# Moving every SBUF tile of a four-layer decoder trunk to a common byte offset, and the split weights to eight others

## The chip, the cores and the metric

The kernel runs on one core of a Trainium2 chip. The metric is the device time of one execution in microseconds (us). Before the change the median of two runs is 2387.1 us (2386.57 and 2387.62). The profile and the rows below come from one further execution of 2388.11 us.

## The reference

A decoder trunk of four pre-norm residual layers works on a sequence of 512 positions with 1024 features, all in float32. Layer i mixes tokens with differential attention (layers 0 and 3), stick-breaking attention (layer 1) or sliding-window attention (layer 2), and each mixer is followed by a gated MLP of 2 x 2752 hidden features with a causal convolution of width 3:

```python
for layer in range(DEPTH):
    h = rmsnorm(x, attn_norm[layer])
    m = mixer(h)                      # qkv = h @ w_qkv, attention
    x = x + m @ w_o[layer]
    h = rmsnorm(x, ffn_norm[layer])
    u = conv(h @ w_up[layer]) + conv_b[layer]
    gate, val = split(u)
    x = x + (silu(gate) * val) @ w_down[layer]
return rmsnorm(x, final_norm)
```

The output is the whole 512 x 1024 array.

## The kernel before

Activations lie transposed: a tile has 128 features as partitions and the 512 positions as columns, so x is eight pieces of 128x512. To keep float32 accuracy with the fp32r matmul, each operand is split into a high part (rounded to fp32r by a copy) and a low part (the rest), and each product is three matmuls: high times high, high times low, low times high. The helper `mm3` (lines 497 to 500) issues them. In it the first operand after the output is the stationary one, loaded as 128x128 weights, and the next is the moving one, streamed through the array, mostly 512 columns.

**The weights** come from HBM in pieces of 128x512 float32 (four 128x128 blocks side by side) through four buffers `w_raw`. For each piece ScalarE writes a copy into one of four buffers `w_hi` (line 288) and VectorE writes the difference into one of four buffers `w_lo` (line 291). The buffers go round in rings, so a high tile and a low tile of the same number serve together, for twelve matmuls as a rule: four blocks times three. The ring order is fixed when the program is written out.

**The stages.** In each layer the q, k and v projections and the attention are interleaved on TensorE. Projections to q and k, and the up-projection of the MLP, move `h_hi` and `h_lo` (the normed x, split) against weights from `w_hi` and `w_lo`. The projections to v (line 561) do it the other way round: `w_hi` and `w_lo` are moved in 256 columns, and blocks of `h_hi` and `h_lo` are the weights. Then `out_projection` (line 1207) moves the attention's output `oh`, `ol`, and `feed_forward` (line 1228) moves the activated hidden features `gh`, `gl`, 21 pieces for each of eight outputs plus a last half piece (`gt_hl` against `wt_hi` and `wt_lo`, lines 1348 and 1349). The last output of the last layer is made in two halves of 256 columns.

**The order of the work** is written out by a planner: `Clock` (line 147) keeps an estimated time for each engine and decides by it in which order instructions are emitted. Its costs do not know addresses.

**Where tiles lie.** `pool.tile` lays the tiles of a pool one behind the other, each size rounded up to 32 bytes; an attention pool and a feed-forward pool take turns in the same space above the constants, and a tile of the new pool may be written only when the last reader of what lay there is done. An address below is bytes within a partition, and an offset is the address modulo 256. In the kernel before:

| tiles | offset |
|---|---|
| `w_raw`, `w_hi`, `w_lo`, `x`, `h_hi`, `h_lo`, `r_bc` | 192 |
| `acc`, `acc_h`, `acc_l`, `ones_r`, `tmp`, `ident`, `sbm` | 224 |
| `oh`, `ol`, `gh`, `gl`, `gt_hl` | 128 |
| `wt_hi`, `wt_lo`, the five `y` | 224 |
| matmul operands inside attention (`qs`, `ql`, `ks`, `vh`, `vl`, `at`) in layers 0, 2 and 3 | 0 |
| matmul operands inside attention (`qs`, `ql`, `ks`, `vh`, `vl`, `ah`, `al`) in layer 1 | 128 |

Blocks and pieces inside a tile are 512 or 2048 bytes apart, so they have their tile's offset.

Of the kernel before, what the change touches and what calls it, by code (L numbers as in the profile page):

```python
# [11 lines left out]
F32 = mybir.dt.float32  # L12
F32R = mybir.dt.float32r
# [4 lines left out]
P = 128  # L18
T = 512
D = 1024  # L20
ND = D // P
NB = T // P
DEPTH = 4
D_FF = 2752
NFF = D_FF // P
# [4 lines left out]
N_BUCKETS = 32  # L30
# [17 lines left out]
def lambda_init(layer):  # L48
    return 0.8 - 0.6 * math.exp(-0.3 * layer)


def f(ap):
    return ap.bitcast(F32)


def flat(ap):
    return ap.rearrange("p k m -> p (k m)")
# [15 lines left out]
def mm(*ns, prio=0):  # L73
    return PE, sum(max(n / 2.4, 107.0) for n in ns), prio


def act(n, prio=0):
    return ACT, 95 + 0.83 * n, prio


def dve(n, ops=1, prio=0):
    return DVE, ops * (70 + 1.04 * n), prio
# [14 lines left out]
def pool_dma(prio=0):  # L97
    return POOL, 1000.0, prio
# [48 lines left out]
class Clock:  # L147
# [7 lines left out]
    def spawn(self, gen):  # L155
        task = Task(gen, self)
        self.todo.append((task, None))
        return task
# [60 lines left out]
def trunk(ctx: ExitStack, tc: tile.TileContext, A, out):  # L219
    nc = tc.nc  # L220

    const = ctx.enter_context(tc.tile_pool(name="const", bufs=1))
# [3 lines left out]
    clock = Clock()  # L226
# [3 lines left out]
    def event():  # L230
        return Event(clock)

    def ring(pool, name, bufs, shape=(P, T), dtype=F32):
        return Ring(clock, [pool.tile(list(shape), dtype, name=f"{name}_{i}") for i in range(bufs)])

    banks = ring(psp, "ps", 8)

    def load_const(name):
        ap = A[name]
        t = const.tile(list(ap.shape), F32, name=f"c_{name}")  # L240
        nc.gpsimd.dma_start(out=t, in_=ap)
        return t

    pinned = "natural_log_exp_and_others"
    nc.scalar.preload_act_table_set(pinned)
    gains = load_const("gains")
    eps = const.tile([P, 1], F32, name="eps")
    nc.vector.memset(eps, EPS)


    stream = []
    raws = ring(const, "w_raw", 4)
    w_hi = ring(const, "w_hi", 4, dtype=F32R)
    w_lo = ring(const, "w_lo", 4, dtype=F32R)
    used = [0]

    def stream_rows(w, pieces):
# [54 lines left out]
        w_lo.give(w[1])  # L312


    xa = const.tile([P, ND, T], F32, name="x")
    x = [xa[:, d, :] for d in range(ND)]
    h_hi = [const.tile([P, T], F32R, name=f"h_hi{d}") for d in range(ND)]
    h_lo = [const.tile([P, T], F32R, name=f"h_lo{d}") for d in range(ND)]
    r_bc = const.tile([P, T], F32, name="r_bc")
    r_col = const.tile([P, NB], F32, name="r_col")  # L320
    acc = const.tile([P, T], F32, name="acc")
    acc_h = const.tile([P, T], F32R, name="acc_h")
    acc_l = const.tile([P, T], F32R, name="acc_l")
    ones_r = const.tile([P, P], F32R, name="ones_r")
    nc.vector.memset(acc[:, 0:P], 1.0 / P)
    nc.vector.tensor_copy(ones_r, acc[:, 0:P])
    tmps = ring(const, "tmp", 3)
# [156 lines left out]
    spawn(w_feed(first))  # L484

    ident = load_const("ident")
    sbm = const.tile([P, 2, P], F32R, name="sbm")
    tri_r, rest_r = (sbm[:, i, :] for i in range(2))
    sinks = const.tile([P, 16], F32, name="sinks")
    nc.gpsimd.dma_start(out=sinks, in_=A["sinks"].to_broadcast([P, 16]))  # L490
    subln = load_const("subln")
    sb_mask = load_const("sb_mask")
# [184 lines left out]

    rows_da = dram.tile([16, DA_Y], F32, name="rows_da")
    rows_sw = dram.tile([16, SW_Y], F32, name="rows_sw")
    neg_lam = const.tile([P, 2], F32, name="neg_lam")  # L680
    neg_sinks = const.tile([P, 16], F32, name="neg_sinks")
    subln_s = const.tile([P, 2], F32, name="subln_s")
    tables = event()

    def setup_tables(pool, big, small):
        def const_in(name, r):
            ap = A[name]
            n = math.prod(ap.shape[1:])
            t = yield r
            v = t if len(t.shape) == 2 else flat(t)  # L690
            yield pool_dma()
            nc.gpsimd.dma_start(out=v[0:ap.shape[0], :n], in_=flat(ap) if len(ap.shape) == 3 else ap)
            return t, v[0:ap.shape[0], :n]

        t0, onehot_da = yield from const_in("onehot_da", big)
        t1, onehot_sw = yield from const_in("onehot_sw", small)
        tab = pool.tile([N_BUCKETS + 1, 16], F32, name="tab")
        yield dve(16)
        nc.vector.memset(tab, 1.0)
        yield pool_dma()  # L700
        nc.gpsimd.dma_start(out=tab[0:N_BUCKETS], in_=A["rel_bias"])
        t2, masks = yield from const_in("sb_masks", small)
        lam_t = yield small
        yield pool_dma()
        nc.gpsimd.dma_start(out=lam_t, in_=A["lam"].to_broadcast([P, 512]))
        yield DMA_LAT
        for rows, oh, n, t, r in ((rows_da, onehot_da, DA_Y, t0, big), (rows_sw, onehot_sw, SW_Y, t1, small)):
            sbt = yield big
            sb = flat(sbt)
            for c in range(0, n, T):  # L710
                e = min(n, c + T)
                ps = yield banks.spare(1)
                yield mm(4 * (e - c), prio=-1)
                nc.tensor.matmul(ps[0:16, 0:e - c], tab, oh[:, c:e], start=True, stop=True)
                yield LAT
                yield dve(e - c)
                nc.vector.tensor_copy(sb[0:16, c:e], ps[0:16, 0:e - c])
                banks.give(ps)
            r.give(t)
            yield pool_dma(-1)  # L720
            nc.gpsimd.dma_start(out=rows, in_=sb[0:16, 0:n])
            clock.t += DMA_LAT
            big.give(sbt)
        yield DMA_LAT
        tables.set()
        yield dve(256)
        nc.vector.tensor_copy(flat(sbm), masks)
        small.give(t2)
        lam = lam_t.rearrange("p (l j e) -> p l j e", l=2, j=4)
        prod_t = yield small  # L730
        prod = prod_t[:, 0:256].rearrange("p (l j e) -> p l j e", l=2, j=2)
        dots = pool.tile([P, 2, 2], F32, name="lam_dots")
        yield dve(128, 2)
        for j in range(2):
            nc.vector.tensor_tensor(prod[:, :, j], lam[:, :, 2 * j], lam[:, :, 2 * j + 1], ALU.mult)
        small.give(lam_t)
        yield dve(256)
        nc.vector.tensor_reduce(dots, prod, mybir.AxisListType.X, ALU.add)
        small.give(prod_t)
        yield act(4)  # L740
        nc.scalar.activation(dots, dots, AF.Exp)
        yield dve(16, 5)
        for s in range(2):
            li = lambda_init(3 * s)
            nc.vector.scalar_tensor_tensor(neg_lam[:, s:s + 1], dots[:, s, 1:2], -li, dots[:, s, 0:1], ALU.add, ALU.subtract)
            nc.vector.tensor_scalar(subln_s[:, s:s + 1], subln[:, s:s + 1], 1.0 - li, None, ALU.mult)
        nc.vector.tensor_scalar(neg_sinks, sinks, -1.0, None, ALU.mult)
# [478 lines left out]


    def feed_forward(pool, l, norm, nxt):
        gh = pool.tile([P, NFF, T], F32R, name="gh")
        gl = pool.tile([P, NFF, T], F32R, name="gl")  # L1230
        gt_hl = pool.tile([P, T], F32R, name="gt_hl")
        gt_l = pool.tile([64, T], F32R, name="gt_l")
        ut = ring(pool, "ut", 3, (P, T + 2))
        for _, _, t in ut.free:
            nc.gpsimd.memset(t[:, 0:2], 0.0)
        y_r = ring(pool, "y", 5)

        wt_hi = pool.tile([P, D], F32R, name="wt_hi")
        wt_lo = pool.tile([P, D], F32R, name="wt_lo")
        nc.gpsimd.memset(f(wt_lo)[64:P], 0.0)  # L1240
        g = [event() for _ in range(NFF)]
        wt = [event(), event()]
# [113 lines left out]
    spawn(norm.finish(True))  # L1356
    for l in range(DEPTH):
        with tc.tile_pool(name=f"att{l}", bufs=1, reuse_waits="tile") as pool:
            oh = pool.tile([P, ND, T], F32R, name="oh")
            ol = pool.tile([P, ND, T], F32R, name="ol")  # L1360
            done, last_bank = [event() for _ in range(ND)], event()
            nxt = Norm(2 * l + 1)
            if l % 3 == 0:
                tasks = diff_attention(pool, norm, l, l // 3, oh, ol, done, last_bank)
            elif l % 3 == 1:
                tasks = stick_attention(pool, norm, l, oh, ol, done, last_bank)
            else:
                tasks = window_attention(pool, norm, l, oh, ol, done, last_bank)
            tasks.append(spawn(out_projection(oh, ol, done, last_bank, nxt, tasks[int(l % 3 != 1)])))
            clock.run(tasks)  # L1370
            norm = nxt
            spawn(norm.finish(False))
        with tc.tile_pool(name=f"ffn{l}", bufs=1, reuse_waits="tile") as pool:
            last = l == DEPTH - 1
            nxt = LastNorm(2 * l + 2) if last else Norm(2 * l + 2)
            clock.run(feed_forward(pool, l, norm, nxt))
            norm = nxt
            if not last:
                spawn(norm.finish(True))
# [94 lines left out]
```

## Time and profile before

| | |
|---|---|
| median of the runs | 2387.1 us |
| profiled execution | 2388.11 us |
| its span, first to last instruction | 2386.3 us |
| TensorE matmul, instructions | 11271 |
| VectorE, ScalarE, GpSimd busy | 1620.2, 1225.1, 382.1 us |
| mean granted TensorE clock | 0.996 |

Matmuls are pipelined: the duration that the profile gives one overlaps the next. How fast TensorE goes through them is read from the distance between the starts of two matmuls in the timeline, divided by the matmuls between them, called the pitch here. The timeline gives starts to 0.01 us, so the pitch is taken over several matmuls.

### The profile page before, as it was taken

Reading aid. Unit: us, or ns where it says so; the run is one execution under the profiler, and the core shown is the slowest. Engines: PE = TensorE matmul, PEld = TensorE weight load, DVE = VectorE, ACT = ScalarE, POOL = GpSimd, SP = SyncE. Lnnn points to the kernel's source line nnn. Section 1 sums busy time; section 2 is a strip of 40 time slices with the busy share of each in tenths; the row PEclk is TensorE's granted clock in tenths of the full one; section 3 lists DMA queues with packets and bytes.
Section 4 is the critical chain, followed back from the end, with each engine's and each line's share of the span. In section 5 each row is a group of like instructions: output and inputs, shape, how many; then the busy total and the mean of one; then the engine's idle time right before and its main releaser. Section 6 shows DMA issues by size and latency. Waiting matters only on the chain.

```text
span 2386.3 us, 33050 instructions
## 1 busy us (share of the span) xinstructions
PE 2337.6 (98%) x11271; PEld 1943.6 (81%) x11271; DVE 1620.2 (68%) x3054; ACT 1225.1 (51%) x2413; POOL 382.1 (16%) x405
## 2 busy tenths in 40 slices
PE   8999999999999999999999899999999999999998
PEld 6888788888877887888888788888888887888887
DVE  6787877743499968777335858776336886877624
ACT  4665545433477755454335855454334665545433
POOL 3343200000144311000002320000012443000001
PEclk9999999999999999999999999999999999999999
DMA  5553333333333323333335423333335642333333
GB/s 188 157 151 94 98 98 106 98 90 92 124 102 93 99 67 98 98 106 94 93 92 151 129 67 104 96 106 93 93 113 143 156 137 71 108 99 103 95 90 108
DMA packets 144153, 256.34 MB, mean 107 GB/s; under 512 B 18511, under 2 KB 33519, under 8 KB 143984
## 3 DMA queue, kind: packets, MB, share of 16 engines
q1 hardware_dynamic: 139856, 241.57, 33.7%
q0 software_dynamic: 4128, 12.66, 2.1%
q8 instruction: 88, 1.44, 0.3%
q14 instruction: 81, 0.66, 0.1%
HBM read 212.15 MB, written 2.16 MB: 90 GB/s over the span
## 4 chain that ended last, share of the span: by engine, by line
PE 59%; DVE 5%; ACT 1%; DMA 1%; issue 1%; POOL 0%; SPq 0%; DVEq 0%; ACTq 0%; POOLq 0%
PE ps L499 18%; PE ps L500 18%; PE ps L498 18%; PE ps L561 2%; PE ps L675 1%; DVE w_lo L291 1%; DMA ks<-lo 1%; DVE h_lo L366 1%; DVE a L799 0%; ACT ns L783 0%; PE ps L1157 0%; DVE ns L779 0%; DVE vl L581 0%; PE ps L992 0%; DVE x L1203 0%
## 5 line engine op out<-in xcount | busy, mean ns | idle before, releaser
L288 ACT ACTIVATE w_hi<-w_raw 128x512 fp32r<-128x512 f32 (+2 forms) x775 | 477.6, 617 | 827.9 <-PE ps L499 665.7
L291 DVE TENSOR_TENSOR w_lo<-w_raw,w_hi 128x512 fp32r<-128x512 f32 (+2 forms) x775 | 538.5, 696 | 444.2 <-ACT w_hi L288 434.2
L498 PE MATMUL ps<-h_hi,w_hi 128*128 128x512 f32 x1840 | 721.9, 392 | 6.7 <-ACT h_hi L364 5.4
L500 PE MATMUL ps<-h_hi,w_lo 128*128 128x512 f32 x1840 | 718.7, 391 | 2.8 <-DVE w_lo L291 2.8
L499 PE MATMUL ps<-h_lo,w_hi 128*128 128x512 f32 x1840 | 720.5, 392 | 0.7
L499 PEld LDWEIGHTS ps<-h_lo,w_hi 128*128 128x128 f32 x1840 | 346.5, 188 | 78.1 <-DVE h_lo L366 9.5
L498 PEld LDWEIGHTS ps<-h_hi,w_hi 128*128 128x128 f32 x1840 | 346.6, 188 | 76.9 <-ACT h_hi L364 5.4
L500 PEld LDWEIGHTS ps<-h_hi,w_lo 128*128 128x128 f32 x1840 | 346.3, 188 | 75.7 <-DVE w_lo L291 3.2
L498 PE MATMUL ps<-gh,w_hi 128*128 128x512 f32 (+1 forms) x693 | 268.4, 387 | 0.0
L500 PE MATMUL ps<-gh,w_lo 128*128 128x512 f32 (+1 forms) x693 | 268.2, 387 | 0.0
L499 PE MATMUL ps<-gl,w_hi 128*128 128x512 f32 (+1 forms) x693 | 268.2, 387 | 0.0
L1249 DVE TENSOR_TENSOR ut<-ps,r_bc 128x512 f32<-128x512 f32 x172 | 118.5, 691 | 176.8 <-PE ps L500 176.8
L381 POOL TENSOR_TENSOR acc<-tmp,tmp 128x512 f32<-128x512 f32 x9 | 11.6, 1292 | 1036.4 <-ACT tmp L373 1032.6
L1254 ACT ACTIVATE y<-ut,c_conv 128x512 f32<-128x512 f32 x172 | 140.2, 815 | 44.0 <-DVE ut L1249 44.0
L499 PEld LDWEIGHTS ps<-gl,w_hi 128*128 128x128 f32 x693 | 129.6, 187 | 30.3
L500 PEld LDWEIGHTS ps<-gh,w_lo 128*128 128x128 f32 x693 | 129.7, 187 | 30.1
L498 PEld LDWEIGHTS ps<-gh,w_hi 128*128 128x128 f32 x693 | 129.6, 187 | 30.0
L1256 DVE SCALAR_TENSOR_TENSOR y<-ut,c_conv,y 128x512 f32<-128x512 f32 x172 | 128.5, 747 | 21.6 <-ACT y L1254 21.4
L1257 DVE SCALAR_TENSOR_TENSOR y<-ut,c_conv,y 128x512 f32<-128x512 f32 x172 | 129.3, 752 | 6.1
L381 POOL TENSOR_TENSOR acc<-acc,tmp 128x512 f32<-128x512 f32 x53 | 76.9, 1451 | 286.8 <-ACT tmp L373 243.1
L561 PE MATMUL ps<-w_hi,h_hi 128*128 128x256 f32 x416 | 119.2, 287 | 0.0
L561 PE MATMUL ps<-w_lo,h_hi 128*128 128x256 f32 x416 | 118.1, 284 | 0.0
(205 smaller groups left out, 3440.3 us busy)
## 6 DMA issues: line engine op xcount, KB each, us to landing
w_raw<-in_w_up_dram SPq DMA_DIRECT2D x344, 256.0 KB, 2.6
w_raw<-in_w_qk_dram SPq DMA_DIRECT2D x108, 256.0 KB, 2.8
w_raw<-in_w_down_dram SPq DMA_DIRECT2D x99, 256.0 KB, 2.6
w_raw<-in_w_down_dram SPq DMA_DIRECT2D x99, 192.0 KB, 2.3
qs<-hi SPq DMA_DIRECT2D x128, 128.0 KB, 3.1
w_raw<-in_w_o_dram SPq DMA_DIRECT2D x64, 256.0 KB, 2.7
w_raw<-in_w_v_dram SPq DMA_DIRECT2D x52, 256.0 KB, 2.8
ql<-lo SPq DMA_DIRECT2D x64, 128.0 KB, 3.0
```

The lines of the kernel that those rows point to most:

```text
L288: copy(hi[:, :n], raw[:, :n], AF.Copy)
L291: nc.vector.tensor_tensor(lo[:, :n], raw[:, :n], f(hi[:, :n]), ALU.subtract)
L366: nc.vector.scalar_tensor_tensor(h_lo[d], x[d], g, f(h_hi[d]), ALU.mult, ALU.subtract)
L381: nc.gpsimd.tensor_tensor(acc, self.first if n == 2 else acc, sq, ALU.add)
L498: nc.tensor.matmul(ps, wh, xh, start=start, stop=False, **kw)
L499: nc.tensor.matmul(ps, wh, xl, start=False, stop=False, **kw)
L500: nc.tensor.matmul(ps, wl, xh, start=False, stop=stop, **kw)
L561: nc.tensor.matmul(dst, a[:, ts], c[:, j, :], start=k + b + n == 0, stop=k == ND - 1 and n == 2, skip_group_check=True)
L1249: nc.vector.tensor_tensor(u[:, 2:T + 2], ps, r, ALU.mult)
L1254: nc.scalar.activation(y, u[:, 2:T + 2], AF.Identity, scale=cw[:, 2:3], bias=cw[:, 3:4])
L1256: nc.vector.scalar_tensor_tensor(y, u[:, 1:T + 1], cw[:, 1:2], y, ALU.mult, ALU.add)
L1257: nc.vector.scalar_tensor_tensor(y, u[:, 0:T], cw[:, 0:1], y, ALU.mult, ALU.add)
```

## The change

A small tile `home` and a helper `place` are new. `home` takes 64 bytes, after which the next address has offset 192. `place` allocates a tile and, behind it, an unused filler that brings the tile's size to a multiple of 256 bytes, so that the next tile has offset 192 again. All SBUF tiles are allocated through it, in the constants and in the pools, but for the eight tiles of split weights. These get unused fillers of 0, 128, 128, 32, 96, 128, 96 and 64 bytes in front of them, in the order of `w_hi` 0 to 3 and `w_lo` 0 to 3, and one of 96 bytes behind the last. Worked out from that, their offsets become:

| | 0 | 1 | 2 | 3 |
|---|---|---|---|---|
| `w_hi` | 192 | 64 | 192 | 224 |
| `w_lo` | 64 | 192 | 32 | 96 |

No instruction is added, removed or reordered; the operands' addresses alone differ. The core of the diff:

```diff
+    const.tile([P, 16], F32, name="home")
+
+    def place(pool, name, shape, dtype=F32):
+        t = pool.tile(list(shape), dtype, name=name)
+        gap = -(-(-4 * math.prod(shape[1:]) // 32) * 32) % 256
+        if gap:
+            pool.tile([P, gap // 4], F32, name=name + "_gap")
+        return t
+
     def ring(pool, name, bufs, shape=(P, T), dtype=F32):
-        return Ring(clock, [pool.tile(list(shape), dtype, name=f"{name}_{i}") for i in range(bufs)])
+        return Ring(clock, [place(pool, f"{name}_{i}", shape, dtype) for i in range(bufs)])
...
     raws = ring(const, "w_raw", 4)
-    w_hi = ring(const, "w_hi", 4, dtype=F32R)
-    w_lo = ring(const, "w_lo", 4, dtype=F32R)
+
+    apart = []
+    for i, gap in enumerate((0, 128, 128, 32, 96, 128, 96, 64)):
+        if gap:
+            const.tile([P, gap // 4], F32, name=f"w_apart{i}")
+        apart.append(const.tile([P, T], F32R, name=f"w_{'hl'[i // 4]}{i % 4}"))
+    const.tile([P, 24], F32, name="w_apart")
+    w_hi, w_lo = Ring(clock, apart[:4]), Ring(clock, apart[4:])
...
-    h_hi = [const.tile([P, T], F32R, name=f"h_hi{d}") for d in range(ND)]
-    h_lo = [const.tile([P, T], F32R, name=f"h_lo{d}") for d in range(ND)]
+    h_hi = [place(const, f"h_hi{d}", (P, T), F32R) for d in range(ND)]
+    h_lo = [place(const, f"h_lo{d}", (P, T), F32R) for d in range(ND)]
...
-        gh = pool.tile([P, NFF, T], F32R, name="gh")
-        gl = pool.tile([P, NFF, T], F32R, name="gl")
-        gt_hl = pool.tile([P, T], F32R, name="gt_hl")
-        gt_l = pool.tile([64, T], F32R, name="gt_l")
+        gh = place(pool, "gh", (P, NFF, T), F32R)
+        gl = place(pool, "gl", (P, NFF, T), F32R)
+        gt_hl = place(pool, "gt_hl", (P, T), F32R)
+        gt_l = place(pool, "gt_l", (64, T), F32R)
...
-            oh = pool.tile([P, ND, T], F32R, name="oh")
-            ol = pool.tile([P, ND, T], F32R, name="ol")
+            oh = place(pool, "oh", (P, ND, T), F32R)
+            ol = place(pool, "ol", (P, ND, T), F32R)
...
```

## Rows read from the trace of the kernel before

**Rows 1.** The page, part 1: busy us (share of the span), instructions.

```profile
PE 2337.6 (98%) x11271; PEld 1943.6 (81%) x11271; DVE 1620.2 (68%) x3054; ACT 1225.1 (51%) x2413; POOL 382.1 (16%) x405
```

**Rows 2.** Waits of TensorE, longest in total: waiter, releaser, us, times, longest.

```profile
PE ps L499 <- DVE al L971: 6.1, 9, 1.9
PE ps L988 <- DVE z L960: 5.4, 9, 1.3
```

**Rows 3.** Groups by line: output<-moving,weights, shape, count, busy us, mean ns, idle before.

```profile
L498 PE MATMUL ps<-h_hi,w_hi 128*128 128x512 f32 x1840 | 721.9, 392 | 6.7 <-ACT h_hi L364 5.4 <-ACT w_hi L288 1.3
L498 PE MATMUL ps<-gh,w_hi 128*128 128x512 f32 (+1 forms) x693 | 268.4, 387 | 0.0
L498 PE MATMUL ps<-oh,w_hi 128*128 128x512 f32 x256 | 102.1, 399 | 0.3 <-DVE nm L1068 0.3
L561 PE MATMUL ps<-w_hi,h_hi 128*128 128x256 f32 x416 | 119.2, 287 | 0.0
```

**Rows 4.** Timeline of TensorE in layer 0's up-projection: start, duration in us.

```profile
300.00 0.39 PE L500 MATMUL ps<-h_hi,w_lo 128*128 128x512 f32 x1
...
301.36 0.39 PE L500 MATMUL ps<-h_hi,w_lo 128*128 128x512 f32 x1
```

**Rows 5.** The same in layer 0's down-projection, also six matmuls apart.

```profile
500.00 0.39 PE L499 MATMUL ps<-gl,w_hi 128*128 128x512 f32 x1
...
501.40 0.39 PE L499 MATMUL ps<-gl,w_hi 128*128 128x512 f32 x1
```

**Rows 6.** The same in layer 0's output projection, six matmuls apart.

```profile
201.21 0.39 PE L498 MATMUL ps<-oh,w_hi 128*128 128x512 f32 x1
...
202.61 0.39 PE L498 MATMUL ps<-oh,w_hi 128*128 128x512 f32 x1
```

**Rows 7.** The same in a projection to v, 256 columns, twelve matmuls apart.

```profile
49.43 0.28 PE L561 MATMUL ps<-w_hi,h_hi 128*128 128x256 f32 x1
...
50.87 0.28 PE L561 MATMUL ps<-w_hi,h_hi 128*128 128x256 f32 x1
```

**Rows 8.** The same in the last half output, 256 columns, six matmuls apart.

```profile
2360.04 0.28 PE L499 MATMUL ps<-gl,w_hi 128*128 128x256 f32 x1
...
2360.72 0.28 PE L499 MATMUL ps<-gl,w_hi 128*128 128x256 f32 x1
```

**Rows 9.** The same where weights at offset 224 come between h's matmuls.

```profile
113.17 0.39 PE L499 MATMUL ps<-h_lo,w_hi 128*128 128x512 f32 x1
113.40 0.40 PE L500 MATMUL ps<-h_hi,w_lo 128*128 128x512 f32 x1
113.64 0.40 PE L846 MATMUL ps<-osh,ones_r 128*128 128x512 f32 x1
...
114.35 0.40 PE L499 MATMUL ps<-h_lo,w_hi 128*128 128x512 f32 x1
```

**Rows 10.** The same where four score matmuls (offset 0) come between h's.

```profile
65.60 0.39 PE L500 MATMUL ps<-h_hi,w_lo 128*128 128x512 f32 x1
65.83 0.39 PE L675 MATMUL ps<-ks,qs 128*128 128x512 f32 x1
...
66.75 0.39 PE L498 MATMUL ps<-h_hi,w_hi 128*128 128x512 f32 x1
```

**Rows 11.** Busy us (instructions) of each engine in 20 us of up- and down-projection.

```profile
300.00:320.00 20.00, 20.00 (x90) 16.57 (x89) 15.05 (x23) 9.25 (x15) 0.00 (x0) 1.00 0.29 92
500.00:520.00 20.00, 20.00 (x87) 16.07 (x86) 6.75 (x11) 6.29 (x11) 0.00 (x0) 1.00 0.35 96
```

**Rows 12.** Timeline of GpSimd where layer 3 begins: start, us, [idle before <-releaser].

```profile
1772.41 0.52 POOL L542 MEMSET ql<- 64x512 f32 x1
1781.20 1.50 POOL L771 DMA_DIRECT2D bias<-rows_da  x2 [8.27 <-PE ps L500]
1785.27 1.28 POOL L381 TENSOR_TENSOR acc<-acc,tmp 128x512 f32<-128x512 f32 x1 [2.57 <-ACT tmp L373]
```

More of the change, by code (lines that the diff above doesn't have):

```diff
@@ L239, in load_const @@
         ap = A[name]
-        t = const.tile(list(ap.shape), F32, name=f"c_{name}")
+        t = place(const, f"c_{name}", tuple(ap.shape))
         nc.gpsimd.dma_start(out=t, in_=ap)
@@ L246, in trunk @@
     gains = load_const("gains")
-    eps = const.tile([P, 1], F32, name="eps")
+    eps = place(const, "eps", (P, 1), F32)
     nc.vector.memset(eps, EPS)
@@ L312, in w_done @@
         w_lo.give(w[1])
-    xa = const.tile([P, ND, T], F32, name="x")
+    xa = place(const, "x", (P, ND, T), F32)
     x = [xa[:, d, :] for d in range(ND)]
-    h_hi = [const.tile([P, T], F32R, name=f"h_hi{d}") for d in range(ND)]
-    h_lo = [const.tile([P, T], F32R, name=f"h_lo{d}") for d in range(ND)]
[L319 to L324, printed above, removed]
+    h_hi = [place(const, f"h_hi{d}", (P, T), F32R) for d in range(ND)]
+    h_lo = [place(const, f"h_lo{d}", (P, T), F32R) for d in range(ND)]
+    r_bc = place(const, "r_bc", (P, T), F32)
+    r_col = place(const, "r_col", (P, NB), F32)
+    acc = place(const, "acc", (P, T), F32)
+    acc_h = place(const, "acc_h", (P, T), F32R)
+    acc_l = place(const, "acc_l", (P, T), F32R)
+    ones_r = place(const, "ones_r", (P, P), F32R)
     nc.vector.memset(acc[:, 0:P], 1.0 / P)
@@ L486, in trunk @@
     ident = load_const("ident")
-    sbm = const.tile([P, 2, P], F32R, name="sbm")
+    sbm = place(const, "sbm", (P, 2, P), F32R)
     tri_r, rest_r = (sbm[:, i, :] for i in range(2))
-    sinks = const.tile([P, 16], F32, name="sinks")
+    sinks = place(const, "sinks", (P, 16), F32)
     nc.gpsimd.dma_start(out=sinks, in_=A["sinks"].to_broadcast([P, 16]))
@@ L679, in trunk @@
     rows_sw = dram.tile([16, SW_Y], F32, name="rows_sw")
-    neg_lam = const.tile([P, 2], F32, name="neg_lam")
-    neg_sinks = const.tile([P, 16], F32, name="neg_sinks")
-    subln_s = const.tile([P, 2], F32, name="subln_s")
+    neg_lam = place(const, "neg_lam", (P, 2), F32)
+    neg_sinks = place(const, "neg_sinks", (P, 16), F32)
+    subln_s = place(const, "subln_s", (P, 2), F32)
     tables = event()
@@ L696, in setup_tables @@
         t1, onehot_sw = yield from const_in("onehot_sw", small)
-        tab = pool.tile([N_BUCKETS + 1, 16], F32, name="tab")
+        tab = place(pool, "tab", (N_BUCKETS + 1, 16), F32)
         yield dve(16)
@@ L731, in setup_tables @@
         prod = prod_t[:, 0:256].rearrange("p (l j e) -> p l j e", l=2, j=2)
-        dots = pool.tile([P, 2, 2], F32, name="lam_dots")
+        dots = place(pool, "lam_dots", (P, 2, 2), F32)
         yield dve(128, 2)
@@ L1236, in feed_forward @@
         y_r = ring(pool, "y", 5)
-        wt_hi = pool.tile([P, D], F32R, name="wt_hi")
-        wt_lo = pool.tile([P, D], F32R, name="wt_lo")
+        wt_hi = place(pool, "wt_hi", (P, D), F32R)
+        wt_lo = place(pool, "wt_lo", (P, D), F32R)
         nc.gpsimd.memset(f(wt_lo)[64:P], 0.0)
```

## The prediction

> **What bounds the kernel now.** I read the page's part 1 first: TensorE's matmuls are busy 98% of the span, VectorE 68%, ScalarE 51%, GpSimd 16% [rows 1]. Since matmuls overlap, 98% alone doesn't say that TensorE is the limit, so the waits come next: the longest two kinds of TensorE's own waits are 6.1 and 5.4 us in total [rows 2], and the big groups of the line table had next to no idle time before them [rows 3]. So the time is the number of matmuls times their pitch, and a change that adds and removes no instruction can only act through the pitch, or through waits for a tile's space.
>
> The third view is the timeline, for the pitch. In the up-projection six matmuls of 512 columns start within 301.36 - 300.00 = 1.36 us, 226.7 ns each [rows 4]. In the down-projection six take 1.40 us, 233.3 ns [rows 5], and in the output projection 1.40 us too [rows 6]. Shape, clock and instruction are the same; VectorE and ScalarE are twice as busy in the quicker stage (15.05 and 9.25 us against 6.75 and 6.29 in 20 us) [rows 11], so crowding by them doesn't explain the 6.7 ns. What differs is where the tiles lie: moving and stationary tile at offset 192 in the first, moving at 128 and stationary at 192 in the other two. Matmuls of 256 columns show the same step the other way round: 1.44/12 = 120 ns with both at 192 [rows 7], 0.68/6 = 113.3 ns with 128 against 192 [rows 8]. So addresses matter here, in steps of 6.7 ns, and no settled row shows a pitch below 226.7 and 113.3. Both are 17/16 of the columns at 2.4 GHz (213.3 and 106.7 ns), though each loads the same 128 columns of weights.
>
> **The change part by part.** The sum is made against the profiled execution, 2388.1 us; the runs' median is 1.0 us lower.
>
> Part 1, `gh` and `gl` go from 128 to 192, where `h_hi` and `h_lo` lie. 31 outputs of 512 columns times 21 pieces are 651 matmuls on each of three lines (the 42 others of the 693 are half outputs [rows 3]), 1,953 in all, at 6.7 ns: -13.0 us, if they settle as the up-projection does. With no effect of the moving tile it is 0.
>
> Part 2, `oh` and `ol`, likewise: 3 x 256 = 768 matmuls [rows 3] at 6.7 ns, -5.1 us, or 0.
>
> Part 3, the projections to v: 3 x 416 = 1,248 matmuls of 256 columns [rows 3], now at 120 ns. Their moving tiles are the ones set apart. The bounds are 0 and 1,248 x 6.7 = -8.3 us (all at 113.3). I take half, -4.2 us, since half of the eight tiles get another offset that is a multiple of 64 or stays, and half of the runs may come to rest at either value.
>
> Part 4, weights at another offset than the tile that moves. This can take back what parts 1 and 2 bring, and it touches also the 3 x 1,840 = 5,520 matmuls on `h` [rows 3], which are at the lower pitch already. The nearest rows differ. Loading `qs` at offset 0 while `h_hi` streams leaves the pitch at 0.23 us [rows 10]; so an offset that differs by a multiple of 64 seems harmless, and sets 0 and 1 of the weights (192, 64, 64, 192) are priced at nothing, with 0 as one end and the 230 ns of the mixed passage below as the other. Loading `ones_r` at 224 does cost: from 113.40 to 114.35 four matmuls take 0.95 us, 237.5 ns each, against 226.7 [rows 9]. Set 3 (224 and 96) is wholly of that kind, 32 past a multiple of 64, and set 2 with its low tile at 32, one load in three. A quarter of the 5,520 + 2,721 matmuls runs on each set, 2,060. The ends for an odd load are 0 (the train settles, as trains do) and 10.8 ns (rows 9 go on). I take 3.3 ns, half of the one step between the two settled pitches, because rows 9 are a passage of two odd loads and the train on set 3 is twelve matmuls long and has time to settle. Set 3: 2,060 x 3.3 = +6.8 us; set 2: a third of it, +2.3 us. Ends: 0 and 22.2 + 7.4 = +29.6 us.
>
> Part 5, matmuls inside attention, from 0 or 128 to 192: four scores at offset 0 take 66.75 - 65.83 = 0.92 us, 230 ns [rows 10], 3.3 above the settled pitch. They come in groups of a few, so I take nothing; the other end is -4 us, an estimate: some 1,260 matmuls, counted from attention's loops, at 3.3 ns.
>
> Part 6, space. The fillers move pool tiles by up to some 5,000 bytes against each other. Worked out from the sizes, `ql` 1 of layer 3 then begins at 209,344 and reaches into `wt_hi` (212,160 on), which layer 2's last matmuls read; before they lay apart. So GpSimd's last two memsets would move from 1772.41 to the end of layer 2, where its bias transfers start at 1781.20 now, waiting for TensorE anyway. Behind them is the sum `acc` at 1785.27, which waits 2.57 us for ScalarE [rows 12]: two memsets of 0.52 us fit in. Cost 0; without that cover, about 1 us. Busy times of the other engines don't count, as TensorE doesn't wait for them. Engine and DMA orders stay as written, and `w_raw`, the target of the large transfers, keeps its offset.
>
> **Sum:** -13.0 - 5.1 - 4.2 + 6.8 + 2.3 = -13.2 us; 2388.1 - 13.2 = 2374.9, and at the median's level **2374 us**, -0.6%. The case's own range runs from all gains without part 4 (-30.4 us, 2357) to the settled gains of parts 1 and 2 with the full price of part 4 (+11.5 us, 2399).
>
> **The rivals.**
>
> Slower: the eight offsets keep every train from settling. The place is the change of tile within each three matmuls (high, high, low), which now changes the offset each time on sets 0 to 2, where before all lay at 192. The price is the mixed passage, 230 ns [rows 10]: 5,520 x 3.3 = +18.2 us, and 2,721 x -3.3 = -9.0 us, together +9 us, 2396. It decides from the pitch p at which 5,520 (p - 226.7) = 2,721 (233.3 - p), p = 228.9 ns. At 235 ns and more, between rows 10 and 9, it would exceed 2%: 8,241 x 6.1 = 50 us. For it: rows 9. Against it: rows 4, where the block changes by 512 bytes within the tile without any mark. Chance 0.20, and 0.03 more for over 2%.
>
> No effect: the pitch differs between stages for another reason than the address, and the time stays at 2387, within 2 us. For it: all `gh` stages differ from all `h` stages in more than the offset. Against it: rows 7 and 8 turn the order round with offsets alone in common with rows 4 and 5. Chance 0.12. By the Trainium skill, "SBUF — State Buffer", section "Who interferes with whom", TensorE has two independent read ports, one for the moving operand and one for weights, and never waits on anyone; by that rule this rival would hold. Rows 4 and 5, 226.7 and 233.3 ns, do not agree with it.
>
> A lower step: with the weights apart, 512 columns go at 220 ns, one step below 226.7, by the same conflict having been there before in all trains. 5,520 x 6.7 + 2,721 x 13.3 = 37 + 36 = 73 us, 2314. For it: steps exist. Against it: rows 4 and 8 both rest at 17/16 of their columns, which a cost of the weights, the same for both widths, wouldn't give. Chance 0.06. The Trainium skill, "TensorE: Matmul & The Clock Gate", section "Wait — 56ns, not 53.3ns?", gives N / 2.4 GHz + 2.5 ns, 215.7 ns for 512 bf16 columns; an estimate by that page for all 8,241 matmuls would be 61 + 48 = 109 us less. No row here shows such a pitch.
>
> **How the numbers follow.** The forecast's case has 0.59, and the rivals 0.20 + 0.03, 0.12 and 0.06. The predicted time is the likeliest case's, 2374. The range of 2354 to 2400 takes in its bounds, the slower rival and no effect, and leaves out the lower step and the slowdown of over 2%, some 0.1 with the edges. Over 2% faster (below 2339) needs the lower step: 0.06. Over 2% slower (above 2435): 0.03. Within 2%, which is about what a measurement of this kernel can tell from no change: 0.91.
>
> **What would show it.** In the changed kernel's timeline, six matmuls on `gh` in the down-projection within 1.36 us confirm part 1, 1.40 refute it; six on `oh` the same for part 2; twelve on line 561 between 1.36 and 1.44 us for part 3. For part 4, twelve matmuls on tiles of set 3 should take longer than on set 0. The memsets of `ql` after 1780 us, with `acc` no later, show part 6. The prediction is wrong if `h`'s six matmuls in the up-projection go much over 1.37 us or below 1.34 us on average.

## The result: 2409.9 us, 1% slower

The changed kernel takes 2409.91 us (median of two runs, 2409.84 and 2409.98) against 2387.1 before, a ratio of 1.0095 with a 95% interval of 1.0071 to 1.012. The forecast was 2374, range 2354 to 2400: wrong in sign and outside the range. The interval excludes 1. The profiled execution has a span of 2408.1 us, 21.8 more than the 2386.3 before.

The page of the changed kernel, part 1, answers to [rows 1]:

```profile
PE 2360.6 (98%) x11271; PEld 1944.9 (81%) x11271; DVE 1624.3 (67%) x3054; ACT 1224.2 (51%) x2413; POOL 382.3 (16%) x405
```

TensorE is busy 23.0 us longer with the same 11,271 matmuls. Its waits, the longest two kinds, answer to [rows 2] and have hardly moved (6.3 and 5.6 us, 6.1 and 5.4 before):

```profile
PE ps L515 <- DVE al L987: 6.3, 9, 1.8
PE ps L1004 <- DVE z L976: 5.6, 9, 1.3
```

So the time went into the pitch and not into waits. The groups by line (output<-moving,weights, shape, count, busy us, mean ns, idle before) show where, against [rows 3]. The weights are now called `w_h` and `w_l`:

```profile
L514 PE MATMUL ps<-h_hi,w_h 128*128 128x512 f32 x1840 | 728.9, 396 | 5.9 <-ACT h_hi L380 5.1 <-ACT w_h L304 0.8
L514 PE MATMUL ps<-gh,w_h 128*128 128x512 f32 (+1 forms) x693 | 268.4, 387 | 0.0
L514 PE MATMUL ps<-oh,w_h 128*128 128x512 f32 x256 | 101.8, 398 | 0.2 <-DVE nm L1084 0.2
L577 PE MATMUL ps<-w_h,h_hi 128*128 128x256 f32 x416 | 117.7, 283 | 0.0
```

On `h` the busy time rose from 721.9 to 728.9 us on one of three such lines. On `gh` it is 268.4 as before, on `oh` 101.8 (102.1 before): the expected gains are not there. On the projections to v it fell by 1.5. A matmul's own duration overlaps its neighbour's, so the pitch has to come from the starts. The timeline of TensorE (start, duration in us) has three stretches here: six matmuls apart in the up-projection, six apart in the down-projection, and six apart in a projection to v. They answer to [rows 4, 5, 7]:

```profile
300.01 0.40 PE L514 MATMUL ps<-h_hi,w_h 128*128 128x512 f32 x1
...
301.41 0.39 PE L514 MATMUL ps<-h_hi,w_h 128*128 128x512 f32 x1
...
519.82 0.39 PE L516 MATMUL ps<-gh,w_l 128*128 128x512 f32 x1
...
521.22 0.40 PE L516 MATMUL ps<-gh,w_l 128*128 128x512 f32 x1
...
49.11 0.28 PE L577 MATMUL ps<-w_h,h_lo 128*128 128x256 f32 x1
...
49.82 0.28 PE L577 MATMUL ps<-w_h,h_lo 128*128 128x256 f32 x1
```

The six on `h` take 1.40 us where they took 1.36; the six on `gh` still take 1.40; six of 256 columns take 0.71, 118.3 ns each against 120. For the whole kernel I took the differences between successive starts and averaged them by the stage of the first of the two matmuls, leaving out those more than 25 ns above 17/16 of the columns at 2.4 GHz (226.7 and 113.3 ns), which end in a wait. The count is of the matmuls that stay in before, in the last row of all; the change in us is of the whole stage, those with waits included:

| matmuls | count | before, ns | after, ns | change, us |
|---|---|---|---|---|
| on `h`, 512 columns | 5,405 | 227.35 | 232.34 | +26.2 |
| on `gh`, `gl` and, 62 of them, `gt_hl`, 512 columns | 2,015 | 233.23 | 232.40 | -1.7 |
| on `oh`, `ol`, 512 columns | 753 | 233.19 | 232.51 | -0.5 |
| projections to v, 256 columns | 1,217 | 119.59 | 118.26 | -2.8 |
| attention and the rest | 1,719 | | | +0.9 |

They add up to +22.1, against 21.8 in the span. One number stands out: in all three groups of 512 columns the pitch is now about 232.4 ns. In what follows, `gh` and `oh` stand for the whole of their rows.

The other engines are no more crowded than before. Busy us of PE, PEld, DVE, ACT and POOL (instructions), the granted clock, the DMA share and GB/s in 20 us of the up-projection, against the first line of [rows 11]:

```profile
300.00:320.00 20.00, 20.00 (x88) 16.17 (x87) 13.77 (x22) 9.43 (x15) 0.00 (x0) 1.00 0.30 103
```

88 matmuls instead of 90 at the same full clock is the slowdown itself, seen in 20 us.

### The profile page after: what moved, and what is told of

It reads as the page before. It is cut to its first block, busy times and chain, and to the rows that moved or that the text cites. A ratio compares the mean times of both kernels' runs of the same rounds, so it can differ in the third digit from the quotient of the medians.

```text
span 2408.1 us, 33051 instructions
## 1 busy us (share of the span) xinstructions
PE 2360.6 (98%) x11271; PEld 1944.9 (81%) x11271; DVE 1624.3 (67%) x3054; ACT 1224.2 (51%) x2413; POOL 382.3 (16%) x405
## 4 chain that ended last, share of the span: by engine, by line
PE 85%; DVE 9%; DMA 2%; issue 2%; ACT 2%; SPq 0%; POOL 0%; DVEq 0%; ACTq 0%; POOLq 0%
PE ps L515 26%; PE ps L516 26%; PE ps L514 25%; PE ps L577 4%; PE ps L691 2%; DVE w_l L307 2%; DMA ks<-lo 1%; DVE u L944 1%; DVE al L987 1%; DVE ah L984 1%; DVE a L815 1%; DVE z L976 1%; DVE sh L947 0%; DVE h_lo L382 0%; PE ps L893 0%
## 5 line engine op out<-in xcount | busy, mean ns | idle before, releaser
L304 ACT ACTIVATE w_h<-w_raw 128x512 fp32r<-128x512 f32 (+2 forms) x775 | 478.0, 617 | 850.0 <-PE ps L515 692.3
L307 DVE TENSOR_TENSOR w_l<-w_raw,w_h 128x512 fp32r<-128x512 f32 (+2 forms) x775 | 539.0, 697 | 445.8 <-ACT w_h L304 438.6
L514 PE MATMUL ps<-h_hi,w_h 128*128 128x512 f32 x1840 | 728.9, 396 | 5.9 <-ACT h_hi L380 5.1
L516 PE MATMUL ps<-h_hi,w_l 128*128 128x512 f32 x1840 | 728.6, 396 | 2.8 <-DVE w_l L307 2.8
L515 PE MATMUL ps<-h_lo,w_h 128*128 128x512 f32 x1840 | 728.9, 396 | 0.6
L515 PEld LDWEIGHTS ps<-h_lo,w_h 128*128 128x128 f32 x1840 | 346.6, 188 | 87.1 <-DVE h_lo L382 9.3
L514 PEld LDWEIGHTS ps<-h_hi,w_h 128*128 128x128 f32 x1840 | 347.2, 189 | 84.3 <-ACT h_hi L380 5.1
L516 PEld LDWEIGHTS ps<-h_hi,w_l 128*128 128x128 f32 x1840 | 346.3, 188 | 83.5 <-DVE w_l L307 3.2
L516 PE MATMUL ps<-gh,w_l 128*128 128x512 f32 (+1 forms) x693 | 269.0, 388 | 0.0
L515 PE MATMUL ps<-gl,w_h 128*128 128x512 f32 (+1 forms) x693 | 268.5, 387 | 0.0
L514 PE MATMUL ps<-gh,w_h 128*128 128x512 f32 (+1 forms) x693 | 268.4, 387 | 0.0
L1272 DVE SCALAR_TENSOR_TENSOR y<-ut,c_conv,y 128x512 f32<-128x512 f32 x172 | 128.6, 748 | 22.1 <-ACT y L1270 22.1
```

The source lines that it names most:

```text
L304: copy(hi[:, :n], raw[:, :n], AF.Copy)
L307: nc.vector.tensor_tensor(lo[:, :n], raw[:, :n], f(hi[:, :n]), ALU.subtract)
L514: nc.tensor.matmul(ps, wh, xh, start=start, stop=False, **kw)
L515: nc.tensor.matmul(ps, wh, xl, start=False, stop=False, **kw)
L516: nc.tensor.matmul(ps, wl, xh, start=False, stop=stop, **kw)
L1272: nc.vector.scalar_tensor_tensor(y, u[:, 1:T + 1], cw[:, 1:2], y, ALU.mult, ALU.add)
```

## The experiments

Offsets are bytes past a multiple of 256, as the tiles were laid out. "Distance" in the expectations and below is the weights' offset minus the moving tile's, modulo 256; so before had distance 0 on `h` and 64 on `gh` and `oh`. All means are worked out as in the table above. The theory was that the pitch is 226.7 ns only where the moving tile and the weights share their offset. The rivals were that each part acts alone by the tile it moves, that only odd multiples of 32 cost, that any spacing between weight tiles costs, and that some distance is better than 0.

**Both halves apart: e1_all192, e2_apart_only.** In e1 everything lies at 192, the weights too:

```
-    for i, gap in enumerate((0, 128, 128, 32, 96, 128, 96, 64)):
+    for i, gap in enumerate((0, 0, 0, 0, 0, 0, 0, 0)):
...
-    const.tile([P, 24], F32, name="w_apart")
```

e2 is the kernel before with only the loop over `apart`, so that only the weights (and what they push along) move.

> All SBUF tiles at offset 192, the eight split-weight tiles too (no fillers between them). Theory spread (a train of matmuls settles only where moving tile and all weight tiles share one offset): h, gh and oh products all settle at 226.7 ns, v projections stay at 120; 2387 - 13 - 5 = 2369 us. Theory rest (the new places of the other tiles cost the time, the weights are free): about 2410 us as in the changed kernel. Theory odd offsets (only weights 32 past a multiple of 64 cost): 2369 us too.

> The kernel before with the fillers between the split-weight tiles alone; all other tiles keep their offsets of before (h 192, gh and oh 128). Theory spread: h products go from 227.3 to about 232.3 ns as in the changed kernel, 5,520 x 5.0 = +27 us, gh and oh near 232.5: 2387 + 27 - 2 = 2411 us. Theory rest: no more than 3 us from 2387. Theory odd offsets: sets 2 and 3 alone cost, h on sets 0 and 1 stays at 226.7; about +10 us, 2397.

Measured: e1 2372.46 us, ratio 0.993 (0.9913 to 0.9946); e2 2409.33, ratio 1.009 (1.0075 to 1.0105). In e1 `h` stays at 227.19 ns, `gh` goes to 226.67 (-13.2 us), `oh` to 227.61 (-4.1 us), v stays at 119.67, and attention takes 3.4 us more (0.6 more in e4 below, whose offsets are the same, so waits differ by that much from one execution to the next); together -14.2, and the span is 14.4 shorter. The timeline of TensorE in e1, six matmuls apart in the up- and the down-projection:

```profile
300.11 0.39 PE L513 MATMUL ps<-h_hi,w_h 128*128 128x512 f32 x1
...
301.47 0.39 PE L513 MATMUL ps<-h_hi,w_h 128*128 128x512 f32 x1
...
519.98 0.39 PE L513 MATMUL ps<-gh,w_h 128*128 128x512 f32 x1
...
521.34 0.39 PE L513 MATMUL ps<-gh,w_h 128*128 128x512 f32 x1
```

Both are 1.36 now. In e2 the up-projection, with nothing else changed in the code, is at 1.40, and the mean on `h` at 232.36 ns (+24.5 us):

```profile
299.97 0.39 PE L505 MATMUL ps<-h_hi,w_l 128*128 128x512 f32 x1
...
301.37 0.40 PE L505 MATMUL ps<-h_hi,w_l 128*128 128x512 f32 x1
```

e1 and the changed kernel differ in nothing but the weights' fillers. So spreading the weights is the whole loss, and setting all other tiles to 192 is a gain of 14 us that the spread took back: after has `gh` at 232.40 against 226.67 in e1, 2,015 x 5.73 = 11.5 us, and `oh` at 232.51 against 227.61, 753 x 4.9 = 3.7 us.

**Is a multiple of 64 harmless? e3_lo64, and is it the distance or the spacing? e4_mult256.** In e3 the four low weight tiles lie at 64 and all else at 192, a distance of 128. In e4 the weights have fillers between them as in the change, but of 256 bytes, so that all stay at 192.

```
e3:  for i, gap in enumerate((0, 0, 0, 0, 128, 0, 0, 0)):   # and 128 bytes behind
e4:  for i, gap in enumerate((0, 256, 256, 256, 256, 256, 0, 0)):
```

> All tiles at 192, but the four low weight tiles at 64, so that every load is at a multiple of 64 and the offset changes in each group of three matmuls (192, 192, 64). Theory spread: nothing settles, pitch 230 to 233 in h, gh and oh: 8,241 x 3.3 to 6.7 above 2369, 2396 to 2424 us. Theory odd offsets: all settle at 226.7, 2369 us.

> All tiles at 192, with fillers of 256 bytes between six of the eight weight tiles: they lie at different distances, all multiples of 256. If offsets count modulo 256 it runs as with all tiles at 192: 2369 us, pitch 226.7 in all three products. If a longer period counts (512 or more), the trains do not settle: 2396 us or more.

Measured: e3 2402.85 us, ratio 1.0065 (1.0044 to 1.0085); e4 2372.08, ratio 0.9939 (0.9921 to 0.9958). e4 is e1 again (`h` 227.22, `gh` 226.67, `oh` 227.61 ns), so room between the tiles costs nothing. e3's down-projection in the timeline of TensorE:

```profile
515.81 0.39 PE L514 MATMUL ps<-gh,w_h 128*128 128x512 f32 x1
516.04 0.40 PE L515 MATMUL ps<-gl,w_h 128*128 128x512 f32 x1
516.27 0.40 PE L516 MATMUL ps<-gh,w_l 128*128 128x512 f32 x1
...
517.20 0.39 PE L514 MATMUL ps<-gh,w_h 128*128 128x512 f32 x1
```

Six take 1.39 us. Single steps of 0.23 us, given to 0.01, don't tell the three kinds apart; the means do. In the down-projections, 651 matmuls each: with `w_h` in use and `w_h` loaded next 226.67 ns; with `w_h` in use and `w_l` loaded next 232.46; with `w_l` in use 234.20. So a distance of 128 costs on each of the two matmuls that it touches, 5.8 and 7.5 ns, 13.3 ns for a group of three, and no train grows used to it.

**The absolute offset: e5_all128.** e1 without the tile `home`, which puts moving tiles and weights at 128:

```
-    const.tile([P, 16], F32, name="home")
```

> All SBUF tiles at offset 128 in place of 192, the weights too. Theory difference (only the distance between moving tile and weights counts, modulo 256): as with all tiles at 192, 2372 us and 226.7 ns in h, gh and oh. Theory place (a moving tile at 192 is quick, one at 128 slow, whatever the weights): 233.3 ns in all three, 8,241 x 6.6 = +54 us, 2427 us.

Measured: 2372.27 us, ratio 0.9938 (0.9922 to 0.9955), with `h` at 227.18, `gh` 226.67, `oh` 227.58 ns. Six on `h` in the up-projection take 1.36:

```profile
300.16 0.39 PE L514 MATMUL ps<-h_hi,w_l 128*128 128x512 f32 x1
...
301.52 0.39 PE L514 MATMUL ps<-h_hi,w_l 128*128 128x512 f32 x1
```

128 is as good as 192, so of these two offsets neither is better in itself: it is the distance that counts.

**All distances: e6_scan1, e7_scan2, e11_scan3.** e1 with fillers around the moving tiles, 256 bytes in all, so that each stage has a constant distance of its own: for `h`, `gh`, `oh` it is 32, 96 and 128 in e6; 160, 192 and 224 in e7; 128, 224 and 0 in e11 (whose expectation counts the 224 as 32, the other way round).

```
e6: +    const.tile([P, 56], F32, name="h_before")
...
    +    const.tile([P, 8], F32, name="h_after")
...
    +        pool.tile([P, 40], F32, name="g_before")
    +        pool.tile([P, 24], F32, name="g_after")
    +            pool.tile([P, 32], F32, name="o_before")
    +            pool.tile([P, 32], F32, name="o_after")
e7: 24/40, 16/48, 8/56 words in the same places;  e11: 32/32, 8/56, none
```

> All tiles at 192 but for h at 160, gh and gl at 96, oh and ol at 64: one constant distance from weights to moving tile in each stage, 32, 96 and 128. Theory difference: each stage settles on a pitch of its own that is constant over all its trains, either 226.7 or 233.3 (a step of 6.7). The theory that any distance other than 0 unsettles a train: 230 to 233 in all three, scattered within each group of three. The lower-step rival: one of the distances gives 220.

> As the scan before it, with h at 32, gh and gl at 0, oh and ol at 224: distances 160, 192 and 224 from moving tile to weights. Theory difference: constant pitches of 226.7 or 233.3 by stage. Any distance other than 0 unsettles: scattered pitches near 230 to 233. Lower step: 220 somewhere.

> All tiles as in e1_all192 (the split weights at 192), but h_hi and h_lo at 64, gh and gl at 224, oh and ol at 192: distances of 128, 32 and 0 from the weights, in the order h, gh, oh by offset 64 against 192, 224 against 192, 192 against 192. Theory (any distance that is not a multiple of 256 costs, and which one it is matters only by a few ns): h and gh each at a mean of 229 to 234 ns per 512-column matmul, oh at 227.6 as in e1; span about 2371.9 + 5,400 x 5.5 ns + 2,015 x 5.5 ns = 2413, from 2400 to 2425. Rival of the lower step (some distance lets a train run below 226.7 ns): h or gh under 226 ns, and the span under 2372. Rival by the tile (the price belongs to h, whatever its distance): oh stays at 227.6, gh at 226.7 and h alone is dear, about 2402.

Measured, one run each: 2415.92, 2408.66 and 2407.93 us. In e7 six on `gh` at distance 192 and six on `h` at 160, in the timeline of TensorE:

```profile
519.85 0.40 PE L515 MATMUL ps<-gh,w_h 128*128 128x512 f32 x1
...
521.22 0.39 PE L515 MATMUL ps<-gh,w_h 128*128 128x512 f32 x1
...
300.07 0.40 PE L515 MATMUL ps<-h_hi,w_h 128*128 128x512 f32 x1
...
301.47 0.39 PE L515 MATMUL ps<-h_hi,w_h 128*128 128x512 f32 x1
```

1.37 and 1.40. The eight distances that are multiples of 32, each with the mean pitch of a stage where it holds throughout (on `gh` without the 62 on `gt_hl`, which has another offset):

| distance | 0 | 32 | 64 | 96 | 128 | 160 | 192 | 224 |
|---|---|---|---|---|---|---|---|---|
| ns | 226.7 | 233.3 | 233.3 | 234.2 | 232.6 | 233.4 | 229.0 | 233.3 |
| stage | e1 `gh` | e6 `h` | before `gh` | e6 `gh` | e11 `h` | e7 `h` | e7 `gh` | e11 `gh` |

Distance 0 lies under all others, and none goes at 220. The stages don't all rest at 226.7 or 233.3 either, as one theory had it: 192 has 229.0. In e11 `oh` at distance 0 has 227.57 ns beside a dear `gh` and `h`. Its timeline, six apart:

```profile
195.13 0.39 PE L515 MATMUL ps<-oh,w_h 128*128 128x512 f32 x1
...
196.49 0.39 PE L515 MATMUL ps<-oh,w_h 128*128 128x512 f32 x1
```

1.36 us: the price goes with the distance and not with the tile. The times follow: against e1, e11 has +27.4 us on `h`, +13.2 on `gh`, 0.0 on `oh`, -1.7 on v and -4.9 in attention and the rest, together 34.0, and its span is 34.3 longer.

**Two offsets among the moving tiles: e8_hlo64, e10_lo_hlo64.** In e8 `h_lo` alone lies at 64; in e10 the low weights too.

```
+    const.tile([P, 32], F32, name="h_mid")      # between h_hi and h_lo
...
+    const.tile([P, 32], F32, name="h_after")
e10 also:  for i, gap in enumerate((0, 0, 0, 0, 128, 0, 0, 0)):   # and 128 bytes behind
```

> All tiles at 192 but for h_lo at 64, so that the moving tile's offset changes in each group of three on h while all weights stay at 192; gh and oh keep one offset. Theory spread, in its wider form (a change of distance between neighbouring matmuls unsettles, whichever operand brings it): h at 231 to 232, gh and oh at 226.7; 2372 + 5,520 x 4 to 5 = 2394 to 2400 us. In its narrow form (only weights count): 2372 us.

> All tiles at 192 but h_lo and the four low weight tiles at 64. On h, the weights that are loaded while a tile streams then have that tile's offset each time (w_hi while h_hi streams, w_lo while h_lo streams, w_hi while h_hi streams), and only the weights already in the array differ in two of three matmuls. Theory loading (only the tile being loaded counts): h settles at 226.7, gh and oh stay unsettled at 231 as with the low weights alone at 64: 2372 + 2,721 x 4.4 = 2384 us. Theory both (the distance of the weights in use counts too, 234 against 226.7 as in the run with low weights at 64): h at (226.7 + 234 + 234)/3 = 231.6 ns, 2372 + 8,241 x 4.7 = 2411 us.

Measured: e8 2398.29 us, ratio 1.0043 (1.0027 to 1.0059); e10 2400.39, ratio 1.0047 (1.0027 to 1.0066). In e8 `gh` and `oh` keep 226.70 and 227.64 ns, and `h` has 232.41. But not by the simple sum: `h_lo`, at distance 128, has 232.87, and `h_hi`, whose weights in use and weights loaded next are both at its own offset, has 232.18 all the same. Its six take 1.40:

```profile
299.65 0.40 PE L515 MATMUL ps<-h_hi,w_h 128*128 128x512 f32 x1
...
301.05 0.40 PE L515 MATMUL ps<-h_hi,w_h 128*128 128x512 f32 x1
```

In e10, two distances at once don't add up: `h` has 231.13 on average, with `h_lo` at 232.98 and `h_hi` at 230.2 whether it uses `w_h` or `w_l`, and the time is neither theory's (2384 and 2411). So a rule for each matmul from its own two distances fits e3, and not e8 and e10, nor the next run. That a train is at its lowest only when all its tiles share an offset holds in all of them.

**Does one tile that is off spoil all trains? e9_one_apart.** Only the last low weight tile lies elsewhere, at 96.

```
-    for i, gap in enumerate((0, 128, 128, 32, 96, 128, 96, 64)):
+    for i, gap in enumerate((0, 0, 0, 0, 0, 0, 0, 160)):
```

> All tiles at 192 but one of the eight weight tiles, the last low one, at 96. Local theory (a train pays while it uses a tile at another offset, and the next train is settled again at once): a quarter of the 8,241 matmuls pays some 5 ns, 2372 + 10 = 2382 us, and twelve matmuls on the other tiles go at 226.7. Spreading theory (one such tile throws the following trains off too): toward 2410 us, few matmuls at 226.7.

Measured: 2381.93 us, ratio 0.9976 (0.9965 to 0.9987). A passage of TensorE's timeline where a train on that tile begins:

```profile
500.71 0.39 PE L514 MATMUL ps<-gh,w_h 128*128 128x512 f32 x1
...
502.07 0.39 PE L514 MATMUL ps<-gh,w_h 128*128 128x512 f32 x1
502.30 0.40 PE L515 MATMUL ps<-gl,w_h 128*128 128x512 f32 x1
502.53 0.40 PE L516 MATMUL ps<-gh,w_l 128*128 128x512 f32 x1
...
504.16 0.39 PE L1364 MATMUL ps<-gt_hl,wt_hi 128*128 128x512 f32 x1
```

Six take 1.36 us up to 502.07; the nine behind take 2.09, 232.2 ns each. By the means on `gl` and `gh`, the tiles taken from the order of the matmuls in the kernel, a matmul has 236.7 ns while that tile is loaded, 232.6 while it is used, 230.8 right behind that, and 226.6 to 226.7 elsewhere: 20 ns more for a group of three. The price sets in with the load of the tile and ends one matmul after its last use. That the expected 2382 us came to the microsecond is in part luck: the groups of 512 columns lost 12.8 us against e1 and not 10, and the projections to v took 2.1 less.

**The version that beats both** is e1 or, as good, e4 and e5: 2372 us, 0.7% under the kernel before and 1.6% under the changed one.

## Why the prediction was wrong

**What bounds the kernel** held. Nothing but the pitch moved: the stages on `h` gave +26.2 us, those of the other large groups -5.0, and the longest waits kept their size. One reading there was off: ScalarE is 1.5 times as busy in the quicker stage (9.25 against 6.29 us) and not twice, which leaves the argument as it is.

**Part 4 is the step that failed**, in three sentences of the prediction. First, "an offset that differs by a multiple of 64 seems harmless", so that sets 0 and 1 were priced at nothing. That was read from 0.23 us in [rows 10], one step, given to 10 ns for an effect of 6.7, of which only the loaded tile lay elsewhere. The trace of before has 27 such steps, `qs` loaded behind a matmul on `h_hi` (leaving out one that ends in a wait): they go from 225 to 236 ns, 228.9 on average, where the same matmul with `h_hi` again behind it has 227.2. One of them shows nothing. e3, wholly of multiples of 64, costs 30 us against e1 (2402.85 - 2372.46), and the table has 232.6 at 128 and 233.3 at 64.

Second, an odd load was priced at 3.3 ns because the train "has time to settle". In e9 one such load costs 20 ns in each group of three, to the end of the train.

Third, the sets: I had paired high and low tiles by their numbers. The two rings each hand out the tile that came free first, and in after, by the tiles' offsets matched to the matmuls in order, they drift apart (high tile 0 with low tile 3, for one). The sign that was named, set 3 slower than set 0, didn't show: where these pairs do occur on `h`, a matmul has 232.8 ns on set 0 (28 groups of three) and 232.6 on set 3 (27), and set 1, priced at nothing, has 232.7 (435). Even the 1,044 matmuls on `h_hi` whose weights in use and weights loaded next are both at 192 have 231.5 ns, and the cheapest of the frequent combinations on `h` has 229.9.

Against +9.1 us forecast for part 4, all 5,405 + 2,015 + 753 matmuls of 512 columns cost about 5.2, 5.7 and 4.9 ns above e1: 27.8 + 11.5 + 3.7 = 43 us.

The evidence for the right answer stood in the prediction. There [rows 4] against [rows 5, 6] had shown the pitch rise with a distance of 64, a multiple of 64, between moving tile and weights. I had read that as a rule on the moving tile in parts 1 and 2 and not applied it to the weights in part 4.

**Parts 1 and 2** were right in cause and size, as e1 shows them alone: -13.2 and -4.1 us against -13.0 and -5.1. In the changed kernel they come to -1.7 and -0.5, because part 4 puts a distance back into the same trains.

**Part 3** brought -2.8 us against -4.2, between its bounds of 0 and -8.3. The pitch makes 1,248 x 1.33 ns = 1.7 us of it, the rest is waits: in e4, with no distance and 119.63 ns, v took 1.6 us less than before all the same, and in e1 0.0. So the spread of the weights brought about 1.7, and the term was more than twice too large. Its 113.3 ns came from six matmuls in [rows 8]; the half outputs on `gh` had 115.40 on average.

**Part 5**, nothing, held within a microsecond: +0.9 with the matmuls of 256 columns on `gh`, less than executions differ by (e1 and e4 above). Most operands inside attention shared an offset before, 0 or 128, so their distance stayed 0.

**Part 6** came as foreseen. The timeline of GpSimd (start, duration, idle before and its releaser), to set against [rows 12]:

```profile
1795.95 0.52 POOL L557 MEMSET ql<- 64x512 f32 x1 [9.35 <-PE ps L1364]
1796.52 0.52 POOL L558 MEMSET ql<- 64x512 f32 x1
1796.99 1.50 POOL L787 DMA_DIRECT2D bias<-rows_da  x2
1800.07 1.27 POOL L397 TENSOR_TENSOR acc<-acc,tmp 128x512 f32<-128x512 f32 x1 [1.57 <-ACT tmp L389]
```

The memsets now wait for TensorE and stand directly before the bias transfers; the sum on `acc` still waits 1.57 us for ScalarE, so they are covered; the cover shrank by 2.57 - 1.57 = 1.0 us, as much as two memsets of 0.52 us take. GpSimd runs one semaphore instruction more than before (319 against 318); beside it no instruction was added.

**The rivals.** The slower one, "the eight offsets keep every train from settling", is what happened, but neither its place nor its price was right. The place was the change of offset within each three matmuls; e6, e7 and e11 have no such change and pay 229 to 234 ns all the same, at one constant distance, wherever that isn't 0. The price was 230 ns, from four scores in [rows 10] whose operands all lie at offset 0, so that it isn't the price of a distance; 232.3 to 232.5 was measured. With 232.4 its own sum is 5,520 x 5.7 - 2,721 x 0.9 = +29 us; measured, +26.2 - 1.7 - 0.5 = +24.0 us, and -2.8 from part 3. Its chance of 0.20 was too small for a case whose cause lay in rows that had been read, [rows 4, 5, 6]. "No effect" is refuted by e1 and the changed kernel, 37 us apart by the weights' offsets alone. By the rule of the Trainium skill, "SBUF — State Buffer", section "Who interferes with whom", that TensorE's two read ports are independent and that it never waits on anyone, there should be no difference; the same matmul has 226.7 and 232.4 ns. The lower step is refuted by the table of distances: none has less than 226.7. The 215.7 ns by "TensorE: Matmul & The Clock Gate" of the Trainium skill, section "Wait — 56ns, not 53.3ns?", stand in no run here.

**What stays open.** Why a distance costs 2 to 8 ns on average, why 192 costs less than the others, and why `h_hi` pays in e8 though only its neighbours' moving tile lies elsewhere, and 231.5 ns in the changed kernel where its own weights share its offset. The runs show when the price is paid, not what in the chip takes the time.

## What to carry to other kernels

Where TensorE is busy throughout and each matmul brings new weights, compare the start-to-start pitch of stages that issue the same instruction; a step of 3% between them can come from how the tiles lie, as here. Putting moving tiles and weights at the same offset modulo 256 was worth 0.7% at no cost but space; a distance that is merely constant was no help (e6). This is one kernel, in fp32r and mostly 512 columns. If an observation says that two tiles should agree in something, apply it to both of them: a change that aligns one side and spreads the other can lose more than it gains. A price of a few ns is read from the mean of many starts, not from one difference that is rounded to 10 ns.

## What the runs showed beside that

Matmuls of 256 columns go the other way. The projections to v have 119.67 ns at distance 0 (e1), 118.26 with the spread of the changed kernel, and 116.85 with `h` at 160 and the weights at 192 (e6); the half outputs on `gh` had 115.40 at distance 64 before, and have 119.92 at 0 in e1. So none of the layouts tried served both widths best; here some 8,300 matmuls of 512 columns outweigh some 1,380 of 256.

The offset itself doesn't matter (e5), nor do fillers of 256 bytes between the tiles (e4). The time of the matmuls in and around attention, though, moves by some us between executions: against before, 3.4 us more in e1, 2.4 in e5 and 0.6 in e4, which lay their tiles alike. So a change of that size there says nothing of the layout.
